# Transposes of the input powers later in TensorE's order, the state space's output products in halves of 64 rows, and a third bank for short products

## The chip, the cores and the metric

The kernel runs on one core of a Trainium2 chip. The metric is the device time of one execution in microseconds (us), the median of several. Engines are named as in the profile: PE is TensorE (PEld its weight loads), DVE is VectorE, ACT is ScalarE, POOL is GpSimd, SP is the engine that issues most DMAs.

## What is computed

A trunk of two layers on x of 512 tokens by 1024 channels. Each layer normalises its input, projects it, and runs three mixers side by side; their outputs are gated, merged and projected back. Cut to what matters here:

```python
for l in range(2):
    h = rmsnorm(x, norm_g[l])
    z = h @ w_in[l]                       # 1024 x 6656
    a_val, a_gate, b_val, b_gate, c_u, c_v, c_gate, gates = split(z)
    ya = s5_mixer(a_val, ...) * silu(a_gate)      # 32 groups x 64 complex states, scan over time
    yb = pool_mixer(b_val, ...) * silu(b_gate)    # means over trailing windows of 2, 4, 8, 16 tokens
    yc = sgu_mixer(c_u, c_v, ...) * silu(c_gate)  # 128 x 128 position mixing
    merged = sum(sigmoid(gates) * (ys @ w_branch[l]))
    x = x + merged @ w_out[l]
return rmsnorm(x, final_norm_g)
```

The kernel runs the scan of `s5_mixer` in blocks of 8 time steps. For that it needs, once for both layers, powers of the state matrix times the input gain (the "input powers", tile `ak`) and powers of a rotation (tables `tlo`, `thi`); then for each of four tiles of eight groups short products for the lags within a block (`psk`), the block states (`pse`) and the outputs (`psy`).

## The kernel before

Every large product is made in three passes of float32r: `hi*hi`, `lo*hi` and `hi*lo` (L104 to L106, helper `step`), so one block of 128 output channels over 1024 inputs is 24 matmuls of 128x512. The weights stream in as items: SP loads a raw tile `wr`, ACT rounds it to `wh` (L156), DVE subtracts to get `wl` (L157); each of the three has three buffers. An item whose PE work is done frees its `wh` and `wl` for the third item after it.

TensorE's order is the order in which the program is recorded. Beside the main stream run "sides": Python generators that record a few instructions, then yield a number of microseconds; `tick` (L132) resumes one when the recorder's own clock, which counts 0.64 for each step of three matmuls (`spend`), has passed that much. The side `s5_side` (L524) of layer 0 first copies tables (`stacked`), then makes the input powers: `input_powers` (L376) has six DVE operations into `ak` tiles (L384 to L387), four PE transposes into the bank `psa` (L390), an ACT copy (L392) and a DMA to HBM, `akd`; then come the rotations (L395), all on POOL, and then the four tiles. Where the side resumes, its PE instructions stand in TensorE's order, and TensorE works in order.

The orders of DVE, ACT, POOL and SP are not written by hand: a scheduler plays the recorded program through a timeline when the kernel is built and sets each engine's order by it, sides at a lower priority. Each engine then works in that order; an instruction that waits holds up all behind it on its engine.

Small tiles of up to 128x256 come from the pool `fs` of 8 buffers (L60, helper `small_spare`): the `ap` tiles of the powers of the state matrix, `ak`, the products `tb` of the rotations (L410), `bt`, the tables `tp`, `rt` and more. A request takes over the buffer of an earlier tile, and its first writer waits until that tile's last reader is done. So the order of the requests in the program decides who waits for whom. Short products share the PSUM pool `pa` (L65): `psb`, `psa`, `psk`, `psy`, `pss`, `psz`.

The main stream of layer 0 around the change is, in blocks of 24 matmuls: the four blocks of `a_val` (tile `u`), three blocks of the pooling branch on the unscaled input (called E1, E2, E3 below, operands `gh`, `gl`), its fourth block (P0, operands `hi`, `lo` of the scaled input `hf`, L670 to L673), four gate blocks G3, G2, G1, G0, each followed by a short product `psb` of three matmuls, then the merge: gate blocks O0, O1, then J0 (four steps on `hi`, `lo` of the pooling outputs `y`), O2, J1 and so on. POOL makes the pooled sums (`xq`, L744 to L748) from `xp` (L734), DVE turns them into `pt` (L751 to L753) and splits them (L434).

Of the kernel before, what the change touches and what calls it, by code (L numbers as in the profile page):

```python
# [13 lines left out]
PSUM = bass.MemoryType.PSUM  # L14

P = 128
# [4 lines left out]
NK = 64  # L21
# [4 lines left out]
GELU_A = 0.044715  # L26
GELU_B = 1.5957691216057308
SIDE = 1000
W_PREP = (75.0, 25.0)
W_OPS = 15.0  # L30
W_STATE = 5.0
W_OUT = 16.0
# [19 lines left out]
def hybrid_trunk(ctx: ExitStack, tc, xT, wi, wbr, wo, wglu, wmisc, pv, rows, gain, slam, sbc, sbt, cst, out):  # L52
    nc = tc.nc
    V, S, G, PE = nc.vector, nc.scalar, nc.gpsimd, nc.tensor
# [7 lines left out]
    bp = ctx.enter_context(tc.tile_pool(name="bp", bufs=1))  # L62
    kp = ctx.enter_context(tc.tile_pool(name="kp", bufs=24))
    pm = ctx.enter_context(tc.tile_pool(name="pm", bufs=4, space=PSUM))
    pa = ctx.enter_context(tc.tile_pool(name="pa", bufs=2, space=PSUM))  # L65
    pe = ctx.enter_context(tc.tile_pool(name="pe", bufs=1, space=PSUM))

    S.preload_act_table(AF.Sigmoid)
# [3 lines left out]
    def nm(s):  # L72
        count[0] += 1
        return f"{s}_{count[0]}"
# [4 lines left out]
    def spare(s="f", dt=F32, shape=(P, T)):  # L79
        return fp.tile(list(shape), dt, tag="f", name=nm(s))  # L80

    def small_spare(s="f", shape=(P, T // 2)):
        return fs.tile(list(shape), F32, tag="fs", name=nm(s))
# [4 lines left out]
    def aux(s="aux"):  # L88
        return pa.tile([P, T], F32, tag="aux", name=nm(s))
# [137 lines left out]
    def keep(s, shape):  # L227
        return cp.tile([P, *shape], F32, name=s)
# [84 lines left out]
    def k_unit(a, eng=V):  # L313
        ar, ai = a
        n = k32()
        eng.tensor_tensor(n, k_mul(ar, ar, eng), k_mul(ai, ai, eng), ALU.add)
        f = k32()
        eng.tensor_scalar(f, n, -0.5, 1.5, ALU.mult, ALU.add)
        return k_mul(ar, f, eng), k_mul(ai, f, eng)
# [46 lines left out]
    def stacked():  # L366
        for h in range(2):
            for r in range(2):
                a, b = slice(64 * r, 64 * r + 64), slice(64 * h, 64 * h + 64)
                for o, x, sign in ((war, apr, 1 - 2 * r), (wai, api, -1)):  # L370
                    S.activation(o[a].rearrange("p j (q h) -> p j h q", h=2)[:, :, h], x[b], AF.Copy, scale=float(sign))
                for o, x, sign in ((kar, kre, 1), (kai, kim, 2 * r - 1)):
                    S.activation(o[a].rearrange("p (q h) -> p h q", h=2)[:, h], x[b], AF.Copy, scale=float(sign))


    def input_powers():  # L376
        kr, ki = (bc(a, 1, NS) for a in (kre, kim))
        ar, ai = apr[:, 0:NS], api[:, 0:NS]
        v = lambda a: a.rearrange("p l s q -> p s l q")
        w = lambda a: a.rearrange("p s (l q) -> p s l q", l=DEPTH)  # L380
        ps = aux("psa")
        for r, (x, y, op) in enumerate(((ar, ai, ALU.subtract), (ai, ar, ALU.add))):
            p0, p1 = (small_spare("ak", (P, NS, W2)) for _ in range(2))
            V.tensor_tensor(p0, kr, x, ALU.mult)  # L384
            V.tensor_tensor(p1, ki, y, ALU.mult)
            ak = small_spare("ak", (P, DEPTH, NS, NQ))
            V.tensor_tensor(v(ak), w(p0), w(p1), op)  # L387
            for l in range(DEPTH):
                i = 2 * l + r
                PE.transpose(ps[:, i * P : (i + 1) * P], ak[:, l].rearrange("p s q -> p (s q)"), ident)  # L390
        t = spare("ak")
        S.activation(t, ps, AF.Copy)  # L392
        nc.sync.dma_start(akd.rearrange("l r p e -> p (l r) e"), t.rearrange("p (i e) -> p i e", i=4))

    def rotations(cn, sn):  # L395
        w = k_unit((cn, sn), G)
        for _ in range(3):
            w = k_unit(k_cmul(w, w, eng=G), G)
        for tab, n in ((tlo, 8), (thi, 8)):
            G.memset(tab[0][:, :, 0:1], 1.0)  # L400
            G.memset(tab[1][:, :, 0:1], 0.0)
            m = 1
            while m < n:
                wr = w[0].unsqueeze(2).to_broadcast([P, W2, m])
                wj = w[1].unsqueeze(2).to_broadcast([P, W2, m])
                tr, ti = tab[0][:, :, 0:m], tab[1][:, :, 0:m]
                ps = []
                for x, y in ((tr, wr), (ti, wj), (tr, wj), (ti, wr)):
                    o = small_spare("tb", (P, W2, m))
                    G.tensor_tensor(o, x, y, ALU.mult)  # L410
                    ps.append(o)
                G.tensor_tensor(tab[0][:, :, m : 2 * m], ps[0], ps[1], ALU.subtract)
                G.tensor_tensor(tab[1][:, :, m : 2 * m], ps[2], ps[3], ALU.add)
                w = k_unit(k_cmul(w, w, eng=G), G)
                m *= 2

    def bc(ap, axis, n):
        a = ap.unsqueeze(axis)
        shape = list(a.shape)
        shape[axis] = n  # L420
        return a.to_broadcast(shape)
# [15 lines left out]
    def flat(a):  # L437
        return a.rearrange("p q k -> p (q k)")
# [4 lines left out]
    tm = keep("tm", (8, P))  # L443
    hst = keep("hst", (8, NK))
# [79 lines left out]
    def s5_side(l, ud, st):  # L524
        uu = bp.tile([P, 4, 8, NK], F32, tag="ba", name=nm("uu"))
        for s in range(NS):
            r = 16 * (NS - 1 - s)
            src = ud.rearrange("n (g c) (s k) -> s c (n g) k", c=16, s=NS)[s]
            nc.sync.dma_start(uu[r : r + 16].rearrange("p n g k -> p (n g) k"), src)
        if l == 0:  # L530
            stacked()
            input_powers()
            yield 3
            rotations(*angle)
        ych = bp.tile([P, 4, T], F32, tag="bb", name=nm("ych"))
        st["ych"] = ych
        for t in range(4):
            w = s5_output(l, t)
            e = s5_input(l, t)
            tcs, tsn, rt = s5_tables(l, t)  # L540
            yield W_PREP[l] if t == 0 else W_OPS
            s5_lags(l, t, w)
            yield W_STATE
            ps = pe.tile([P, 2, 4, NK], F32, tag="pe", name=nm("pse"))
            for r in range(2):
                for i in range(4):
                    for h in range(2):
                        PE.matmul(ps[64 * h : 64 * h + 64, r, i], e[r][:, 2 * i + h], uu[:, t, 2 * i + h], start=True, stop=True)  # L548
            sr, si = flat(ps[:, 0]), flat(ps[:, 1])

            def mul(x, y, eng=V):
                o = small_spare("p5")
                eng.tensor_tensor(o, x, y, ALU.mult)  # L553
                return o

            a, b = mul(sr, tcs), mul(si, tsn)
            G.tensor_tensor(a, a, b, ALU.add)  # L557
            d, c = mul(si, tcs), mul(sr, tsn)
            V.tensor_tensor(d, d, c, ALU.subtract)
            gr, gi = small_spare("g5"), small_spare("g5")  # L560
            V.tensor_tensor_scan(gr, rt, a, 0.0, ALU.mult, ALU.add)
            V.tensor_tensor_scan(gi, rt, d, 0.0, ALU.mult, ALU.add)
            b, c = mul(gi, tsn, G), mul(gr, tsn, G)
            a, d = mul(gr, tcs), mul(gi, tcs)
            v3 = lambda z: z.rearrange("p (q k) -> p q k", q=4)[:, :, 0 : NK - 1]
            for r, (x, y, op) in enumerate(((a, b, ALU.subtract), (d, c, ALU.add))):
                for h in range(2):
                    o = hst[64 * r : 64 * r + 64].rearrange("p (q h) k -> p h q k", h=2)[:, h, :, 1:NK]
                    i = slice(64 * h, 64 * h + 64)
                    V.tensor_tensor(o, v3(x)[i], v3(y)[i], op)  # L570
            yield W_OUT
            py = aux("psy")
            for g in range(8):
                o = py[:, g * NK : (g + 1) * NK]
                PE.matmul(o, tm[:, g], uu[:, t, g], start=True, stop=False)  # L575
                PE.matmul(o, w[:, g, 16 : 16 + P], hst[:, g], start=False, stop=True)  # L576
            sq = spare("sq")
            S.activation(sq, py, AF.Square)
            V.tensor_scalar(sq, sq, GELU_A, 1.0, ALU.mult, ALU.add)
            V.tensor_tensor(sq, sq, py, ALU.mult)  # L580
            S.activation(sq, sq, AF.Sigmoid, scale=GELU_B)
            V.tensor_tensor(sq, py, sq, ALU.mult)
            yd = dp.tile([P, T], F32, tag="yd", name=nm("yd"))
            nc.sync.dma_start(yd, sq)
            for g in range(8):
                src = yd.rearrange("(s c) (g k) -> g c s k", c=16, g=8)[g]
                nc.sync.dma_start(ych[16 * g : 16 * g + 16, t].rearrange("p (s k) -> p s k", s=NS), src)
# [474 lines left out]
    with tc.high_priority(offset=-SIDE), tc.issue_after(norms[0].last[1]):  # L1062
        angle = discretise()
# [90 lines left out]
```

## Time and profile before

| | |
|---|---|
| median of 3 runs | 936.67 us (936.38 to 936.79) |
| the profiled execution | 937.1 us |
| its span in the profile | 935.3 us, so 1.8 us lie around it |
| PE busy | 890.3 us, 95% of the span |
| DVE, ACT, POOL busy | 579.1, 299.6, 227.9 us |
| granted TensorE clock, mean | 0.979 of full speed |

Of the page's 40 slices of 23.4 us PE is busy for 4 tenths in the second and third, for 6 tenths in the last and for 8 or more in all others. A busy PE is not PE at its peak: matmuls are pipelined, and their ends are modelled. So starts are compared below: two matmuls of 128x512 that follow each other start 0.227 us apart at full clock (0.43 us at half).

### The profile page before, as it was taken

To read this page: it belongs to the slowest core of one execution; us is meant where nothing else is said; L and a number is where in the kernel's file an instruction comes from. 1 tells how busy PE (TensorE), PEld (TensorE's weight loads), DVE (VectorE), ACT (ScalarE), POOL (GpSimd) and SP (SyncE) were. 2 spreads that over 40 slices of the span, in tenths; PEclk is the share of its full clock that TensorE was granted. 3 is DMA by queue.
4 is the path that set the end of the run, shared out by engine and by line. 5 is a ranking of instruction groups with operands and counts; after the bars stand their busy time and mean duration, and the time that the engine had idled before them with its cause. 6 is when DMAs were issued, how large, how long until landed. Compare 5 with 4: busy or idle time off the path is not lost.

```text
span 935.3 us, 11781 instructions
## 1 busy us (share of the span) xinstructions
PE 890.3 (95%) x4396; PEld 732.0 (78%) x4396; DVE 579.1 (62%) x934; ACT 299.6 (32%) x440; POOL 227.9 (24%) x353
## 2 busy tenths in 40 slices
PE   9449899999999999999999999999999999999996
PEld 5338688888888888888888788887888888888885
DVE  7875662787867776445547787566883435634632
ACT  5232322232222234333433333232322223433521
POOL 1068970213324340000230720201220111000020
PEclk9769899999999999999999999999999999999998
DMA  6823223453324444234225624354422332332402
GB/s 238 172 46 104 68 90 98 147 169 119 119 84 134 131 125 134 90 90 135 91 92 153 127 83 145 98 182 140 145 90 83 101 103 90 103 98 86 155 23 90
DMA packets 65704, 106.85 MB, mean 114 GB/s; under 512 B 30176, under 2 KB 32864, under 8 KB 65648
## 3 DMA queue, kind: packets, MB, share of 16 engines
q1 hardware_dynamic: 65008, 104.88, 37.6%
q0 software_dynamic: 352, 1.10, 0.4%
q8 instruction: 34, 0.56, 0.2%
q14 instruction: 22, 0.18, 0.1%
q10 hardware_dynamic: 288, 0.14, 0.1%
HBM read 99.01 MB, written 7.08 MB: 113 GB/s over the span
## 4 chain that ended last, share of the span: by engine, by line
PE 84%; DVE 8%; POOL 3%; DMA 2%; issue 2%; ACT 1%; SPq 0%; DVEq 0%; ACTq 0%
PE mm L104 23%; PE mm L105 23%; PE mm L106 23%; PE mm L1019 2%; PE mm L1020 2%; PE mm L1021 2%; PE mm L838 1%; PE mm L839 1%; PE mm L840 1%; PE psy L576 1%; PE psy L575 1%; POOL xq L744 1%; PE pse L548 1%; DVE wl L157 1%; PE mm L1015 1%
## 5 line engine op out<-in xcount | busy, mean ns | idle before, releaser
L104 PE MATMUL mm<-hi,wh 128*128 128x512 f32 x960 | 378.2, 394 | 1.0 <-ACT hi L672 1.0
L105 PE MATMUL mm<-lo,wh 128*128 128x512 f32 x960 | 374.8, 390 | 0.5 <-DVE lo L673 0.4
L106 PE MATMUL mm<-hi,wl 128*128 128x512 f32 x960 | 374.4, 390 | 0.1
L157 DVE TENSOR_TENSOR wl<-wr,wh 128x1024 fp32r<-128x1024 f32 (+1 forms) x174 | 200.4, 1152 | 155.7 <-ACT wh L156 155.3
L156 ACT ACTIVATE wh<-wr 128x1024 fp32r<-128x1024 f32 (+1 forms) x174 | 160.2, 921 | 416.7 <-PE mm L105 261.8
L104 PEld LDWEIGHTS mm<-hi,wh 128*128 128x128 f32 x960 | 180.8, 188 | 40.3 <-issue 1.9
L106 PEld LDWEIGHTS mm<-hi,wl 128*128 128x128 f32 x960 | 180.7, 188 | 38.5 <-DVE wl L157 0.5
L105 PEld LDWEIGHTS mm<-lo,wh 128*128 128x128 f32 x960 | 180.7, 188 | 38.3 <-DVE lo L673 0.8
L794 DVE TENSOR_TENSOR sg<-sg,mm 128x512 f32<-128x512 f32 x48 | 32.8, 684 | 44.4 <-PE mm L106 44.4
L796 POOL TENSOR_TENSOR sg<-sg,sg 128x512 f32<-128x512 f32 x16 | 25.2, 1577 | 101.7 <-DVE sg L794 101.7
L609 POOL TENSOR_TENSOR sq<-sq,sq 128x512 f32<-128x512 f32 x7 | 12.7, 1811 | 127.5 <-ACT sq L603 116.6
L104 PE MATMUL mm<-gh,wh 128*128 128x512 f32 x96 | 38.8, 405 | 0.1
L105 PE MATMUL mm<-gl,wh 128*128 128x512 f32 x96 | 38.1, 397 | 0.6 <-DVE gl L599 0.6
L106 PE MATMUL mm<-gh,wl 128*128 128x512 f32 x96 | 38.0, 396 | 0.4 <-DVE wl L162 0.4
L94 ACT ACTIVATE hi<-sg 128x512 fp32r<-128x512 f32 x32 | 20.2, 631 | 33.3 <-DVE sg L796 13.5
L557 POOL TENSOR_TENSOR p<-p,p 128x256 f32<-128x256 f32 x8 | 5.9, 739 | 91.2 <-DVE p L553 91.1
L785 ACT ACTIVATE sg<-mm 128x512 f32<-128x512 f32 x48 | 27.8, 579 | 0.0
L390 PE MATMUL psa<-cs,ak 128*128 128x128 f32 x4 | 1.3, 440 | 27.6 <-DVE ak L387 27.6
L95 DVE TENSOR_TENSOR lo<-sg,hi 128x512 fp32r<-128x512 f32 x32 | 22.0, 687 | 6.5 <-ACT hi L94 6.4
L838 PE MATMUL mm<-wh,hi 128*128 128x512 f32 x64 | 25.5, 398 | 0.2 <-DVE sg L794 0.2
L1019 PE MATMUL mm<-wh,hi 128*128 128x512 f32 x64 | 25.3, 396 | 0.0
L870 POOL TENSOR_TENSOR sg<-sg,z 128x512 f32<-128x512 f32 x8 | 14.6, 1820 | 44.1 <-DVE z L862 44.1
(207 smaller groups left out, 1064.9 us busy)
## 6 DMA issues: line engine op xcount, KB each, us to landing
wr<-in_wi SPq DMA_DIRECT2D x102, 512.0 KB, 3.2
wr<-in_wbr SPq DMA_DIRECT2D x48, 256.0 KB, 2.6
wr<-in_wo SPq DMA_DIRECT2D x16, 512.0 KB, 3.8
ai<-akd SPq DMA_DIRECT2D x16, 256.0 KB
bi<-in_sbt SPq DMA_DIRECT2D x16, 256.0 KB, 4.9
x<-in_xT SPq DMA_DIRECT2D x8, 256.0 KB, 5.2
ud<-u SPq DMA_DIRECT2D x8, 256.0 KB, 2.0
uu<-ud SPq DMA_DIRECT2D x16, 128.0 KB, 6.7
```

The costliest lines, as they stand in the source:

```text
L94: S.activation(hi, src, AF.Copy)
L95: V.tensor_tensor(lo, src, hi.bitcast(F32), ALU.subtract)
L104: PE.matmul(ps, whi[:, k], x[0], start=k == 0, stop=False)
L105: PE.matmul(ps, whi[:, k], x[1], start=False, stop=False)
L106: PE.matmul(ps, wlo[:, k], x[0], start=False, stop=k == n - 1)
L156: S.activation(hi, raw, AF.Copy)
L157: V.tensor_tensor(lo, raw, hi.bitcast(F32), ALU.subtract)
L785: S.activation(sg[m], ps, AF.Sigmoid)
L794: V.tensor_tensor(g, g, ps, ALU.mult)
L796: (V if last is not None else G).tensor_tensor(g, g, macc[m], ALU.add)
L838: PE.matmul(ps, th, w(wh), start=j == 0 and k == 0, stop=False)
L1019: PE.matmul(ps, th, w(wh), start=j == 0 and k == 0, stop=False)
```

## The change

Three edits, and the waits of the side's generator retuned with them.

1. In layer 0's side the rotations are recorded before the input powers, and the input powers only 32 of the recorder's microseconds later (`W_POWERS`); the wait before the first tile's lag products falls from 75 to 30.
2. The pool `pa` gets a third bank.
3. The output products `psy` are made in halves: instead of two products of 128 output rows for each of 8 groups, four of 64 rows. There are 8 such steps of 8 groups (four tiles, two layers).

```diff
--- before.py
+++ after.py
@@ -26,7 +26,8 @@
 GELU_A = 0.044715
 GELU_B = 1.5957691216057308
 SIDE = 1000
-W_PREP = (75.0, 25.0)
+W_POWERS = 32.0
+W_PREP = (30.0, 25.0)
 W_OPS = 15.0
 W_STATE = 5.0
 W_OUT = 16.0
@@ -62,7 +63,7 @@
     bp = ctx.enter_context(tc.tile_pool(name="bp", bufs=1))
     kp = ctx.enter_context(tc.tile_pool(name="kp", bufs=24))
     pm = ctx.enter_context(tc.tile_pool(name="pm", bufs=4, space=PSUM))
-    pa = ctx.enter_context(tc.tile_pool(name="pa", bufs=2, space=PSUM))
+    pa = ctx.enter_context(tc.tile_pool(name="pa", bufs=3, space=PSUM))
     pe = ctx.enter_context(tc.tile_pool(name="pe", bufs=1, space=PSUM))
 
     S.preload_act_table(AF.Sigmoid)
@@ -529,9 +530,10 @@
             nc.sync.dma_start(uu[r : r + 16].rearrange("p n g k -> p (n g) k"), src)
         if l == 0:
             stacked()
+            rotations(*angle)
+            yield W_POWERS
             input_powers()
             yield 3
-            rotations(*angle)
         ych = bp.tile([P, 4, T], F32, tag="bb", name=nm("ych"))
         st["ych"] = ych
         for t in range(4):
@@ -571,9 +573,12 @@
             yield W_OUT
             py = aux("psy")
             for g in range(8):
-                o = py[:, g * NK : (g + 1) * NK]
-                PE.matmul(o, tm[:, g], uu[:, t, g], start=True, stop=False)
-                PE.matmul(o, w[:, g, 16 : 16 + P], hst[:, g], start=False, stop=True)
+                for h in range(2):
+                    o = py[64 * h : 64 * h + 64, g * NK : (g + 1) * NK]
+                    PE.matmul(o, tm[:, g, 64 * h : 64 * h + 64], uu[:, t, g], start=True, stop=False)
+                for h in range(2):
+                    o = py[64 * h : 64 * h + 64, g * NK : (g + 1) * NK]
+                    PE.matmul(o, w[:, g, 16 + 64 * h : 80 + 64 * h], hst[:, g], start=False, stop=True)
             sq = spare("sq")
             S.activation(sq, py, AF.Square)
             V.tensor_scalar(sq, sq, GELU_A, 1.0, ALU.mult, ALU.add)
```

Lines of the changed kernel are up to five higher than those before (the transposes L390 are L391, the pooling L744 is L749).

**TensorE, from the end of layer 0's fourth `a_val` block (`mm_564`).** Before, the transposes stand right behind it, ahead of E1 (`mm_705`):

```order
L106 MATMUL mm_564<-gh_188,wl_465 128x512
L104 MATMUL mm_564<-gh_194,wh_464 128x512
L105 MATMUL mm_564<-gl_195,wh_464 128x512
L106 MATMUL mm_564<-gh_194,wl_465 128x512
L390 MATMUL psa_679<-cs,ak_684 128x128 x2
L390 MATMUL psa_679<-cs,ak_692 128x128 x2
L104 MATMUL mm_705<-gh_146,wh_520 128x512
L105 MATMUL mm_705<-gl_147,wh_520 128x512
L106 MATMUL mm_705<-gh_146,wl_521 128x512
```

With the change they stand behind G2 and its short product, ahead of G1 (`mm_1294`):

```order
L107 MATMUL mm_1230<-hi_639,wl_1138 128x512
L105 MATMUL psb_1258<-hi_1082,hi_1029 128x512
L106 MATMUL psb_1258<-lo_1083,hi_1029 128x512
L107 MATMUL psb_1258<-hi_1082,lo_1030 128x512
L391 MATMUL psa_1268<-cs,ak_1273 128x128 x2
L391 MATMUL psa_1268<-cs,ak_1281 128x128 x2
L105 MATMUL mm_1294<-hi_597,wh_1182 128x512
L106 MATMUL mm_1294<-lo_598,wh_1182 128x512
L107 MATMUL mm_1294<-hi_597,wl_1183 128x512
```

So 144 matmuls of 128x512 (E1 to E3, P0, G3, G2) and two short products moved ahead of the transposes. The first lag products moved from behind 468 large matmuls to behind 408.

**DVE, around the six operations that make `ak`** (the waits name the semaphore, by engine). Before, they follow the last steps of the discretisation:

```order
L363 TENSOR_TENSOR kim<-k_432,inv_417 128x32 [waits DVE_49]
L384 TENSOR_TENSOR ak_680<-kre,apr_107 128x256 [waits DVE_49]
L385 TENSOR_TENSOR ak_681<-kim,api_108 128x256 [waits DVE_49]
L387 TENSOR_TENSOR ak_684<-ak_680,ak_681 128x8x2x16 [waits DVE_49]
L384 TENSOR_TENSOR ak_688<-kre,api_108 128x256
L385 TENSOR_TENSOR ak_689<-kim,apr_107 128x256
L387 TENSOR_TENSOR ak_692<-ak_688,ak_689 128x8x2x16 [waits DVE_49]
L487 TENSOR_TENSOR w_363_1062<-war,sbc_1054 128x576 [waits DMAHW2_49,Activation_49]
L488 TENSOR_TENSOR m_364_1063<-wai,sbc_1054 128x576 [waits Activation_49]
```

With the change they follow the outputs of G3 and G2, and the first and the third of them wait for POOL:

```order
L654 TENSOR_TENSOR sg_1255<-sg_1255,mm_1230 128x512 [waits Activation_49]
L772 SCALAR_TENSOR_TENSOR y_1262<-psb_1258,pvt,sg_1255 128x512 [waits DVE_49,PE_49]
L96 TENSOR_TENSOR lo_1265<-y_1262,hi_1264 128x512 [waits Activation_49]
L385 TENSOR_TENSOR ak_1269<-kre,apr_107 128x256 [waits Pool_49]
L386 TENSOR_TENSOR ak_1270<-kim,api_108 128x256
L388 TENSOR_TENSOR ak_1273<-ak_1269,ak_1270 128x8x2x16 [waits DVE_49,Pool_49]
L385 TENSOR_TENSOR ak_1277<-kre,api_108 128x256
L386 TENSOR_TENSOR ak_1278<-kim,apr_107 128x256 [waits DVE_49]
L388 TENSOR_TENSOR ak_1281<-ak_1277,ak_1278 128x8x2x16 [waits DVE_49]
L478 TENSOR_TENSOR bt_1335<-sbc_1333,kar 128x128 [waits DMAHW1_49,PE_49]
L479 TENSOR_TENSOR bt_1336<-sbc_1333,kai 128x128 [waits Pool_49]
L488 TENSOR_TENSOR w_420_1341<-war,sbc_1333 128x576
```

Their buffers in `fs` are now taken over from the rotations' products `tb`: in the built program the first `ak` waits for L413 of POOL's second round on `thi` (tile 128x64), the third for L414 behind it, and the `bt` operation L479 for the third round (128x128). Before it was the other way round: `tb` waited for `ak`.

**POOL, at the start of the rotations** (the products L232 of `k` tiles, L233 with the change). Before, the rotations stand right behind the norm's `rs`, and the pooled sums `xq` stand among them:

```order
L412 TENSOR_TENSOR tlo_112<-tb_847,tb_849 128x32 [waits Pool_49]
L413 TENSOR_TENSOR tlo_113<-tb_851,tb_853 128x32 [waits Pool_49]
L309 TENSOR_TENSOR k_857<-k_859,k_861 128x32 [waits Pool_49]
L232 TENSOR_TENSOR k_864<-k_841,k_843 128x32
L232 TENSOR_TENSOR k_866<-k_843,k_841 128x32
L744 TENSOR_TENSOR xq_733<-xp_730 128x7x64 [waits DVE_49]
L745 TENSOR_TENSOR xq_733<-xp_730 128x64
L310 TENSOR_TENSOR k_858<-k_864,k_866 128x32 [waits Pool_49]
L232 TENSOR_TENSOR k_870<-k_857 128x32
L744 TENSOR_TENSOR xq_737<-xq_733 128x6x64 [waits Pool_49]
```

With the change all pooled sums of layer 0 stand first, then four memsets of tiles of layer 1, and then the rotations:

```order
L749 TENSOR_TENSOR xq_1169<-xp_1166 128x7x64 [waits Activation_49,Pool_49]
L750 TENSOR_TENSOR xq_1169<-xp_1166 128x64 [waits Pool_49]
L736 MEMSET xp_4685 128x8 [waits DVE_49]
L746 MEMSET xq_4688 128x8
L746 MEMSET xq_4692 128x8 [waits DVE_49,Pool_49]
L736 MEMSET xp_4747 128x8
L233 TENSOR_TENSOR k_680<-k_370 128x32
L233 TENSOR_TENSOR k_682<-k_362 128x32
L317 TENSOR_TENSOR k_679<-k_680,k_682 128x32 [waits Pool_49]
```

The third of those memsets waits until DVE has done L758 (before L753) on the last of the four `pt`. The rotations stand behind it.

## Rows read from the trace of the kernel before

**Rows 1.** The page: span, and a group of part 5 (xcount | busy us, mean ns).

```profile
span 935.3 us, 11781 instructions
...
L157 DVE TENSOR_TENSOR wl<-wr,wh 128x1024 fp32r<-128x1024 f32 (+1 forms) x174 | 200.4, 1152 | 155.7 <-ACT wh L156 155.3
```

**Rows 2.** Waits of PE: engine line waited for: us in total, times, longest us.

```profile
PE psa L390 <- DVE ak L387: 27.6, 2, 27.1
PE psb L104 <- DVE y L767: 4.1, 1, 4.1
```

**Rows 3.** Timeline of PE, 32 to 127 us: start us, us, engine line op xcount [idle before].

```profile
32.42 0.39 PE L106 MATMUL mm<-gh,wl 128*128 128x512 f32 x1
59.90 0.66 PE L390 MATMUL psa<-cs,ak 128*128 128x128 f32 x2 [27.09 <-DVE ak L387]
...
61.39 0.78 PE L104 MATMUL mm<-gh,wh 128*128 128x512 f32 x1
...
67.91 0.39 PE L104 MATMUL mm<-gh,wh 128*128 128x512 f32 x1
...
126.77 0.50 PE L105 MATMUL mm<-lo,wh 128*128 128x512 f32 x1
```

**Rows 4.** Timeline of DVE, 33 to 61 us.

```profile
33.20 0.74 DVE L670 SCALAR_TENSOR_TENSOR hf<-x,pvt,rstd 128x512 f32<-128x512 f32 x1
...
50.32 0.68 DVE L673 TENSOR_TENSOR lo<-hf,hi 128x512 fp32r<-128x512 f32 x1
...
55.77 0.18 DVE L232 TENSOR_TENSOR k<-api,lam 128x32 f32<-128x32 f32 x1
...
58.50 0.41 DVE L384 TENSOR_TENSOR ak<-kre,apr 128x256 f32<-128x256 f32 x1
...
60.57 0.43 DVE L387 TENSOR_TENSOR ak<-ak,ak 128x256 f32<-128x256 f32 x1
```

**Rows 5.** Timeline of DVE, 74 to 86 us.

```profile
76.44 1.58 DVE L157 TENSOR_TENSOR wl<-wr,wh 128x1024 fp32r<-128x1024 f32 x1
...
83.37 1.01 DVE L752 TENSOR_TENSOR xq<-xq,cs 128x16 f32<-128x16 f32 x1
...
85.39 1.09 DVE L434 TENSOR_TENSOR lo<-pt,hi 128x512 fp32r<-128x512 f32 x1 [0.76 <-ACT hi L433]
```

**Rows 6.** Timeline of POOL, 53 to 117 us.

```profile
53.27 0.50 POOL L232 TENSOR_TENSOR k<-k 128x32 f32<-128x32 f32 x2 [24.76 <-DVE k L232]
...
68.60 0.27 POOL L410 TENSOR_TENSOR tb<-tlo,k 128x32 f32<-128x32 f32 x1
...
112.42 0.25 POOL L309 TENSOR_TENSOR k<-k,k 128x32 f32<-128x32 f32 x1
...
113.38 0.44 POOL L232 TENSOR_TENSOR k<-k 128x32 f32<-128x32 f32 x2
...
114.96 0.31 POOL L410 TENSOR_TENSOR tb<-thi,k 128x64 f32<-128x64 f32 x1
...
116.43 0.32 POOL L412 TENSOR_TENSOR thi<-tb,tb 128x64 f32<-128x64 f32 x1
```

**Rows 7.** Timeline of PE around the first `pse` and `psy` steps.

```profile
162.65 0.39 PE L106 MATMUL mm<-hi,wl 128*128 128x512 f32 x1
162.97 0.69 PE L548 MATMUL pse<-uu,e 128*64 128x64 f32 x16
...
164.05 0.50 PE L104 MATMUL mm<-hi,wh 128*128 128x512 f32 x1
164.39 0.39 PE L105 MATMUL mm<-lo,wh 128*128 128x512 f32 x1
...
183.00 0.39 PE L106 MATMUL mm<-hi,wl 128*128 128x512 f32 x1
183.23 0.33 PE L575 MATMUL psy<-uu,tm 128*128 128x64 f32 x2
...
187.03 0.40 PE L839 MATMUL mm<-wl,hi 128*128 128x512 f32 x1
```

## The prediction

> **What bounds the kernel now.** I read the page first, then the waits of PE, then the timelines of PE, DVE and POOL where PE stands. The span is 935.3 us [rows 1], the profiled execution 937.1; the sum below is made against the latter, and the median of the runs lies 0.4 lower. PE is the bound: its waits after the start are two that matter, 27.6 us before the transposes `psa` and 4.1 us before one short product `psb` [rows 2]. In its timeline the reader sees the last matmul of the `a_val` blocks start at 32.42, nothing until the transposes at 59.90, and then 24 matmuls that take 6.52 us (61.39 to 67.91) where 24 at 0.227 take 5.45 [rows 3]: the clock is at its lower level at first, which costs 1.1 us. The other end of this wait is DVE's: from 33.20 it splits the scaled input (last `lo` at 50.32) and beside it computes the powers of the state matrix, and makes `ak` from 58.50 to 61.0 [rows 4]. E1 to E3 need none of this, yet stand behind the transposes. So the first edit takes away a wait that is plainly there. What it costs is the question, since the six `ak` operations get new neighbours.
>
> **When `ak` comes now.** Until L758 on the last `pt`, DVE has its old work and 25 operations that stood behind `ak` before. The old work, from 33.20 to the product L232 of `api` and `lam` that is done at 55.95 [rows 4], is 22.75 us. Moved ahead of that are 6 `wl` (1.15 us in the mean [rows 1], up to 1.58 [rows 5]), 3 `xp`, 4 `pt`, 3 `lo` and the `lo` of `wq` (each a pass over 128x512 like the `lo` of 0.68 [rows 4]; the pooled `lo` up to 1.09 [rows 5]), 4 corrections of 16 columns (0.2 like other small operations [rows 4], up to 1.01 beside POOL [rows 5]) and 4 small `pt` (0.2). All low that is 6.9 + 11 x 0.68 + 8 x 0.2 = 16.0; all high 9.5 + 8 x 0.68 + 3 x 1.09 + 4.0 + 0.8 = 23.0. POOL works on `xq` for about half of that time, and most of these operations keep their duration then, so I take 18. DVE also waits 0.5 for E1, whose result is there at 38.3 (32.65 + 5.45 + 0.2) when DVE would take it at 37.9 by its old pace. That gives 55.95 + 18 + 0.5 = 74.5 (72.5 to 79.5).
>
> Only then POOL's held memset is free, and the rotations begin at 74.7, where before they began at 53.27 [rows 6]. The first `ak` waits for their second round on `thi`. Where DVE leaves POOL alone, normalising a rotation takes 1.58 (113.38 to 114.96) and squaring and normalising 3.05 (112.42 to 114.96, and half a microsecond for the first pair, which stands beside other work there); the round of 64 columns takes 1.8 to its L412 (114.96 to 116.75) [rows 6], 4.6 in all. By these, and 0.3 less and 0.7 more for 32 and 128 columns, the way to the release is 1.58 + 3 x 3.05 for the start, then 4.3 + 4.6 + 5.3 for `tlo`, 4.3 and 1.8 for `thi`: 31.0 us. In the trace of before the start alone, 10.7 by this, took 15.3 (53.27 to 68.60 [rows 6]), beside a DVE that worked nearly all the time: 1.43 times as long, and 44.3 for the whole if that held throughout. It should not hold: with the change DVE has only some 12 us of work left before it stands at `ak` itself, and then nothing disturbs POOL. I add 2.2 for those 12 us and take 33.2, nearest to the undisturbed rows. The release comes at 107.9, and the six `ak`, 2.5 us as now (58.50 to 61.0 [rows 4]), are done at 110.4.
>
> **What PE makes of it.** E1 to E3 run from 32.65 at full pace, P0 waits for the last `lo` (some 6 us later than now, at about 57), G3 and G2 follow, and PE stands before the transposes at about 70: a wait of 40 us for 31.7 before. From the end of `ak`: 0.4 to the first matmul and 6.5 for G1 (as E1 behind the same transposes, 61.0 to 61.39 to 67.91 [rows 3]), 0.7 for its `psb`, 5.45 for G0, 0.7, and 10.9 for O0 and O1: 24.65 us, so J0 starts at 135.0. Before, it started at 126.5 (its second matmul waits until 126.77 [rows 3]). From there PE has work without a gap in both kernels, so the first edit costs **8.5 us**. I cost what lies behind `ak` on DVE at nothing: the lag tables, the first input tiles through HBM and the outputs of G1 and G0 must be ready for J0, and by the same durations they are some 2 us early in those 24.65; three more would show as a wait of 1. The third bank costs nothing and removes the wait of 4.1, which is for a bank that `y` still held; that is in the two start times already. The shorter `W_PREP` brings the lag products 60 matmuls nearer; they come 16 us after J0, behind tables that are finished by then.
>
> **The output products.** A `psy` step now is 32 passes (8 of the rows of 2, for each operand) and takes 3.58: from 183.00 to 187.03, less two matmuls of 0.227 [rows 7]. A `pse` step has passes of the new shape, 64 columns by 64, the halves in turn: 32 of them from 162.97 to 164.05, 1.08, and 1.29 with the gaps on both sides (162.65 to 164.39, less two matmuls) [rows 7]. The new `psy` has 64: 1.29 + 1.08 = 2.37. Eight steps gain 8 x 1.21 = **9.7 us**, all on PE's path. Ends: no gain at all if a half pass costs half of the present 0.11, and at best 18.3 if a step fell to `pse`'s 1.29; `pse` is the same shape and order, so I take its pace.
>
> The sum is 8.5 - 9.7 = -1.2 us: 935.9 for the profiled execution, 935.5 as a median.
>
> **The rivals.**
> *The halves overlap less over a long step* (slower). A step of 64 passes is twice as long as any run of such passes in this trace, and what stands queued at its start may hide the loads of 32 but not of 64. If loads set the pace, two halves cost what one whole does, 0.11 a pair, and `psy` stays at 3.5: the gain is nil, and 8.5 us remain: 945.2. It decides at a pace of 0.054 a pass; `pse` at 0.034 speaks against it, its shortness leaves it open. The Trainium skill, "TensorE: Matmul & The Clock Gate", section "LDWEIGHTS (loading the stationary operand)", says that a load takes its number of columns divided by 1.2 in nanoseconds; an estimate by that page is 64 loads of 53 ns, 3.4 us a step, so nearly this case. By that rule, `pse` would take 1.7 where the trace has 1.08 [rows 7], so the loads of the two halves overlap at least there.
> *POOL stays as slow as before* (slower). At 1.43 times its undisturbed pace throughout the rotations take 44.3, `ak` is done at 121.5, J0 starts 19.6 late, and the sum is +9.9: 946.6. For it: POOL was slow wherever it ran beside DVE [rows 6]; against it: DVE stands still from about 86.
> *The transposes do not wait for POOL* (much faster). If the buffers came free earlier, DVE would go on at about 86, `ak` would be done at 88.5 and J0 start 13.4 early: -23 with the halves, 913.6. Against it stand the waits in the built order; POOL would have to do 31 us of work in 12.
>
> **How the numbers follow.** The forecast has a chance of 0.62, the halves without gain 0.15, the slow POOL 0.13, no wait for POOL 0.05; 0.05 is left for what I don't see. The forecast's own range comes from the start of the rotations (72.5 to 79.5), their pace (31 upwards) and a step of `psy` between 2.2 and 2.8: 930.5 to 941. To hold 8 in 10 the range goes up into the two slower rivals: 930.5 to 945.5. A difference of 0.2%, 1.9 us, is about what a measurement of this kernel can tell from none. The forecast lies within it, near its lower side: of its 0.62, I put 0.26 to faster, 0.22 to no change and 0.14 to slower. The slower rivals add 0.22 to slower and 0.06 to the others, the fast one and half of the rest go to faster. That is 0.36 faster, 0.28 no change, 0.36 slower.
>
> **What would show it.** PE's waits have one long one, about 40 us, before the transposes, by DVE's `ak`; DVE's first `ak` stands some 20 us waiting for POOL's L413; POOL begins the rotations at about 75 and runs faster from 86 on; J0's first matmul is near 135; the wait of 4.1 before `psb` is gone; a `psy` step takes about 2.4. The prediction is wrong if `ak` is done before 100 or after 118, or if a `psy` step is near 3.5.

## The result and the profile after

The changed kernel takes 941.46 us as the median of 4 runs (941.37 to 944.0), the kernel before beside it 936.54 (936.38 to 936.79). The ratio is 1.0059 with a 95% interval of 1.0041 to 1.0076: slower by 4.9 us, where 1.2 us less were forecast. The profiled execution took 941.43 us, its span is 939.6, which is 4.3 more than before [rows 1]. Lines of the page, with the slices of PE and of its granted clock:

```profile
span 939.6 us, 12276 instructions
...
PE 882.9 (94%) x4652; PEld 719.5 (77%) x4652; DVE 578.1 (62%) x934; ACT 299.9 (32%) x440; POOL 216.0 (23%) x353
...
PE   9981199999999999999999999999999999999996
...
PEclk9986599999999999999999999999999999999998
```

In the row of PE the gap is now in one piece, slices 4 and 5, and the clock row shows 6 and 5 tenths of full speed granted there. PE is busy for 882.9 us, 7.4 less than before. The waits of PE (engine line waited for: us in total, times, longest):

```profile
PE psa L391 <- DVE ak L388: 38.8, 2, 38.2
PE mm L105 <- ACT hi L677: 2.8, 4, 1.0
PE mm L106 <- DVE lo L678: 1.4, 3, 0.8
PE mm L107 <- DVE wl L158: 1.3, 1, 1.3
PE mm L843 <- DVE sg L799: 1.2, 1, 1.2
```

Against [rows 2] the wait of 4.1 before `psb` is gone, and that before `psa` has grown from 27.6 to 38.8. DVE's timeline says what `ak` waited for:

```profile
88.12 0.80 DVE L96 TENSOR_TENSOR lo<-y,hi 128x512 fp32r<-128x512 f32 x1 [0.69 <-ACT hi L95]
110.96 0.53 DVE L385 TENSOR_TENSOR ak<-kre,apr 128x256 f32<-128x256 f32 x1 [22.03 <-POOL thi L413]
...
113.28 0.43 DVE L388 TENSOR_TENSOR ak<-ak,ak 128x256 f32<-128x256 f32 x1
...
117.01 0.53 DVE L479 TENSOR_TENSOR bt<-sbc,kai 128x128 f32<-128x128 f32 x1 [3.05 <-POOL thi L413]
```

DVE is done with all else at 88.9, and then stands 22 us before the first `ak`, for POOL's `thi`. Where before `ak` was done at 61.0 [rows 4], it is now at 113.71. The same stretch of POOL:

```profile
72.96 0.11 POOL L746 MEMSET xq<- 128x8 f32 x1
77.72 0.11 POOL L746 MEMSET xq<- 128x8 f32 x1 [4.64 <-DVE pt L758]
...
77.81 0.93 POOL L233 TENSOR_TENSOR k<-k 128x32 f32<-128x32 f32 x2
...
110.60 0.32 POOL L413 TENSOR_TENSOR thi<-tb,tb 128x64 f32<-128x64 f32 x1
```

A memset waits at 77.72 for the last `pt` of DVE, the rotations begin behind it at 77.81 (53.27 before [rows 6]), and the round that releases `ak` ends at 110.92, 33.1 us later. On PE this gives:

```profile
73.93 0.39 PE L107 MATMUL psb<-hi,lo 128*128 128x512 f32 x1
112.53 0.69 PE L391 MATMUL psa<-cs,ak 128*128 128x128 f32 x2 [38.22 <-DVE ak L388]
...
114.10 0.78 PE L105 MATMUL mm<-hi,wh 128*128 128x512 f32 x1
...
118.51 0.63 PE L106 MATMUL mm<-lo,wh 128*128 128x512 f32 x1
118.94 0.44 PE L107 MATMUL mm<-hi,wl 128*128 128x512 f32 x1
...
121.99 0.39 PE L105 MATMUL psb<-hi,hi 128*128 128x512 f32 x1
...
128.11 0.39 PE L105 MATMUL psb<-hi,hi 128*128 128x512 f32 x1
...
139.67 0.39 PE L105 MATMUL mm<-hi,wh 128*128 128x512 f32 x1
```

PE has run E1 to E3, P0, G3 and G2 by 74.3. The row at 112.53 is the transposes, 114.10 the first matmul of G1, 118.51 and 118.94 the last two that start at the half-clock spacing of 0.43; 121.99 and 128.11 are the `psb` of G1 and G0, 139.67 is J0. Before, J0's first matmul stood at 126.31 and its second waited until 126.77 [rows 3]; I count its start as 126.5, one matmul ahead of the second. So everything up to J0 costs 13.2 us.

The output products, to be held against [rows 7]:

```profile
182.39 0.39 PE L107 MATMUL mm<-hi,wl 128*128 128x512 f32 x1
182.70 0.34 PE L578 MATMUL psy<-uu,tm 128*64 128x64 f32 x4
182.87 0.29 PE L581 MATMUL psy<-hst,w 128*64 128x64 f32 x4
...
184.50 0.29 PE L581 MATMUL psy<-hst,w 128*64 128x64 f32 x4
184.72 0.50 PE L105 MATMUL mm<-hi,wh 128*128 128x512 f32 x1
185.05 0.39 PE L106 MATMUL mm<-lo,wh 128*128 128x512 f32 x1
```

The 64 passes stand in groups of four, 0.117 apart, so 0.029 a pass; all eight steps show the same. From 182.39 to 185.05, less two matmuls of 0.227, a step takes 2.21 where it took 3.58: 1.37 less, eight times 11.0. After J0 the waits of PE come to 4.9 us (1.3 + 1.2 + 1.0 + 0.9 + 0.5), before to 2.4. So the difference adds up: 13.2 - 11.0 + 2.5 = 4.7, where the spans differ by 4.3.

### The profile page after: what moved, and what is told of

The parts are those of the page before. It is cut to its first block, busy times and chain, and to the rows that moved or that the text cites. A ratio compares the mean times of both kernels' runs of the same rounds, so it can differ in the third digit from the quotient of the medians.

```text
span 939.6 us, 12276 instructions
## 1 busy us (share of the span) xinstructions
PE 882.9 (94%) x4652; PEld 719.5 (77%) x4652; DVE 578.1 (62%) x934; ACT 299.9 (32%) x440; POOL 216.0 (23%) x353
## 4 chain that ended last, share of the span: by engine, by line
PE 86%; DVE 6%; POOL 3%; DMA 2%; issue 2%; ACT 1%; SPq 0%; DVEq 0%; ACTq 0%
PE mm L105 24%; PE mm L106 24%; PE mm L107 24%; PE mm L1024 2%; PE mm L1025 2%; PE mm L1026 2%; PE mm L843 1%; PE mm L844 1%; PE mm L845 1%; DVE wl L158 1%; POOL k L233 1%; PE pse L550 1%; DVE hf L675 1%; PE psy L578 1%; PE psz L865 1%
## 5 line engine op out<-in xcount | busy, mean ns | idle before, releaser
L158 DVE TENSOR_TENSOR wl<-wr,wh 128x1024 fp32r<-128x1024 f32 (+1 forms) x174 | 198.4, 1141 | 159.8 <-ACT wh L157 159.2
L391 PE MATMUL psa<-cs,ak 128*128 128x128 f32 x4 | 1.4, 447 | 38.8 <-DVE ak L388 38.8
L391 PEld LDWEIGHTS psa<-cs,ak 128*128 128x128 f32 x4 | 0.6, 202 | 39.6 <-DVE ak L388 39.6
L843 PE MATMUL mm<-wh,hi 128*128 128x512 f32 x64 | 25.4, 397 | 1.2 <-DVE sg L799 1.2
L844 PE MATMUL mm<-wl,hi 128*128 128x512 f32 x64 | 25.1, 392 | 0.9 <-DVE wl L158 0.9
```

Of the source, the lines that this page charges most:

```text
L158: V.tensor_tensor(lo, raw, hi.bitcast(F32), ALU.subtract)
L843: PE.matmul(ps, th, w(wh), start=j == 0 and k == 0, stop=False)
L844: PE.matmul(ps, th, w(wl), start=False, stop=False)
```

## Experiments

Ratios are to the kernel before, run beside it on the same chip (its medians there were 936.0 to 936.6).

**The three edits one by one.** First the halves alone:

```diff
+                for h in range(2):
+                    o = py[64 * h : 64 * h + 64, g * NK : (g + 1) * NK]
+                    PE.matmul(o, tm[:, g, 64 * h : 64 * h + 64], uu[:, t, g], start=True, stop=False)
...
```

> The kernel before with nothing changed but the psy step in halves of 64 rows. By the traces of before and of the change a psy step with its gaps went from 3.58 to 2.21 us, 1.37 less, and there are eight: theory one (the halves are a pure gain on TensorE's path, and the late waits of the changed kernel come from its new order) gives 936.5 - 11.0 = 925.5. Rival (the halves bring the 2.5 us of late waits of the changed kernel with them, because the products that follow come sooner): 928. Rival (a step that is faster only in the changed kernel's places, nil here): 936.5.

928.24 us, ratio 0.992 (0.9897 to 0.9944). The runs lie between 926.7 and 931.7, so the interval is wide; the profiled one has a span of 924.9, 10.4 below before, and its waits of PE are those of before but for some 0.5 us. A step takes 2.21 here too. So the halves are worth 11.0 us of TensorE's path, and the time keeps most of it. A product of the second layer (L841, on DVE's `sg`, at 628.7) waits 1.2 us, where before the longest such wait was 0.2; so one of the late waits comes with the halves, as the first rival has it. Its reason is another one, though: in this trace DVE first stands 6.6 us for an input tile from HBM (`ai`, at 621.39) and does the last operation on it (L466) just ahead of that `sg`, where before it ended 8.4 us ahead of it.

Then the new order with the third bank, and `psy` whole (the third edit undone):

> The changed kernel with its psy step whole again: new order and third bank alone. Theory one (J0 starts 13.2 us later because ak waits for POOL's rotations, and the order brings 2.5 us of late waits): 936.5 + 13.2 + 2.5 = 952, with J0's first matmul near 139.7. If the late waits belong to the halves: 949.7. If the order itself costs nothing and the halves are what is slow: 937 or less.

948.12 us, ratio 1.0119 (1.0104 to 1.0135): 11.5 us slower. The wait before `psa` is 39.5, and J0 starts near 138.5 (the second `psb` behind the transposes is at 126.95, and 0.68 and 48 matmuls of 0.227 lie between). So the order is what costs: 12.0 us at J0, 10.7 in the span (946.0 against 935.3). It brings no more late waits by itself (2.1 us after J0, 2.4 before), so 949.7 was the nearest of the three. In the spans the order and the halves alone come to 10.7 - 10.4 = 0.3 us, together they cost 4.3. Of the 4.0 between, 1.2 is the later J0 (the lower clock, see below), 1.5 are longer waits for `wl` after it; the rest wasn't followed.

Then the third bank alone on the kernel before:

```diff
-    pa = ctx.enter_context(tc.tile_pool(name="pa", bufs=2, space=PSUM))
+    pa = ctx.enter_context(tc.tile_pool(name="pa", bufs=3, space=PSUM))
```

> The kernel before with a third bank for short products and nothing else. If the wait of 4.1 us before psb at 102 to 106 is a wait for a bank that y holds, it goes, and with it some 1 us of lower clock behind it: J0 near 121.5 and 931.5. Rival (the bank is held by a chain that the next product meets as well, so the wait moves by one place): 936.5, with a wait of 3 to 5 us before the following psb or J0.

936.85 us, ratio 1.0005 (0.9996 to 1.0015): nothing. The rival is right, and the trace shows the new place. The waits of PE, then DVE's timeline, then three rows of DVE in the kernel before:

```profile
PE psa L390 <- DVE ak L387: 27.5, 2, 27.0
PE mm L104 <- ACT hi L94: 5.2, 1, 5.2
```

```profile
112.71 0.75 DVE L767 SCALAR_TENSOR_TENSOR y<-psb,pvt,sg 128x512 f32<-128x512 f32 x1
116.66 0.39 DVE L477 TENSOR_TENSOR bt<-sbc,kar 128x128 f32<-128x128 f32 x1 [3.21 <-POOL thi L412]
...
122.09 0.74 DVE L767 SCALAR_TENSOR_TENSOR y<-psb,pvt,sg 128x512 f32<-128x512 f32 x1
125.38 1.17 DVE L95 TENSOR_TENSOR lo<-y,hi 128x512 fp32r<-128x512 f32 x1 [2.54 <-ACT hi L94]
```

```profile
105.26 0.75 DVE L767 SCALAR_TENSOR_TENSOR y<-psb,pvt,sg 128x512 f32<-128x512 f32 x1
...
116.79 0.40 DVE L477 TENSOR_TENSOR bt<-sbc,kar 128x128 f32<-128x128 f32 x1 [3.20 <-POOL thi L412]
...
122.23 0.74 DVE L767 SCALAR_TENSOR_TENSOR y<-psb,pvt,sg 128x512 f32<-128x512 f32 x1
```

No `psb` waits any more, but J0 waits 5.2 us for the `hi` of the last `y`. On DVE a `bt` stands 3.2 us for POOL's `thi`, and the `y` that J0 needs comes behind it, at 122.09. In the kernel before, the same `bt` stands as long and the same `y` comes at 122.23; J0 lost only 0.2 to it there, as the wait for the bank, which a `y` at 105.26 ended, had already held TensorE up. So there are two waits one behind the other, the second for POOL's rotations, and the third bank takes away the first alone.

**Taking away the wait for POOL.** In the changed kernel, the six tiles of `ak` come from the pool of full-size tiles, so their buffers are not those of the rotations' products:

```diff
-            p0, p1 = (small_spare("ak", (P, NS, W2)) for _ in range(2))
+            p0, p1 = (spare("ak")[:, 0:256].rearrange("p (s w) -> p s w", s=NS) for _ in range(2))
...
-            ak = small_spare("ak", (P, DEPTH, NS, NQ))
+            ak = spare("ak")[:, 0:256].rearrange("p (l s q) -> p l s q", l=DEPTH, s=NS)
```

> The changed kernel, but the six tiles of ak come from the pool of full-size spare tiles, so that DVE no longer waits for POOL's products of the rotations. Theory one (this wait is what makes the order costly): ak is done near 84 where it was done at 113.7, TensorE's long wait falls from 38.2 to about 10 us, J0 starts near 111 and, if the lag products find their tables in time, the time is 941.5 - 28 = 913; POOL's tables may come late then, for up to 7 us: 913 to 920. Rival (POOL's rotations are the true end of this stage, and the wait only moves on to the lag and state products): 935 to 941.

917.23 us, ratio 0.9791 (0.9776 to 0.9805): 24 us faster than the changed kernel, 19 faster than before. Its waits:

```profile
PE psa L391 <- DVE ak L388: 9.9, 2, 9.4
PE mm L105 <- ACT wh L157: 3.1, 1, 3.1
PE mm L107 <- DVE wl L158: 2.5, 2, 2.1
```

The wait before `psa` has fallen from 38.2 to 9.4. From the first lag products to the first state products TensorE now takes 11.8 us (126.21 to 137.99) where it took 6.3 (156.08 to 162.36): 3.6 of the 5.5 are waits for `wh` and `wl`, the rest is lower clock behind them; the other 2.1 for a `wl` come at 325.0. This run settles the main question: the order was costly because of the shared buffers, and the end of POOL's rotations was no bound of its own.

The rest of that wait goes when `bt` and `rt` come from the same pool. First on the kernel before with its third bank:

```diff
-        p0, p1 = (small_spare("bt", (P, 4, 2, 16)) for _ in range(2))
+        p0, p1 = (spare("bt")[:, 0:128].rearrange("p (i h c) -> p i h c", i=4, h=2) for _ in range(2))
...
-        rt = small_spare("rt", (P, 4, NK))
+        rt = spare("rt")[:, 0 : 4 * NK].rearrange("p (q k) -> p q k", q=4)
```

> The kernel before with the third bank, and with the tiles bt and rt taken from the pool of full-size spare tiles. With the third bank alone the wait of 4.1 us before psb went and one of 5.2 before J0 came, for the last y, which stands on DVE behind a bt that waits for POOL's rotations. If that is what held y in both kernels: J0 starts some 5.6 us of waits and 1 us of lower clock earlier, 930 us. Rival (y is late by DVE's own work): 935 to 937.

929.61 us, ratio 0.9926 (0.9911 to 0.994). J0 no longer waits for `hi`; the only wait left there is 1.1 us for a `lo`. So bank and tiles together are worth 6.5 us, where the bank alone was worth nothing; the tiles alone weren't run.

The same two tiles on the kernel of `ak` from spare tiles:

> The kernel of ak from full-size spare tiles (917.2 us), with bt and rt from there as well, so that neither DVE nor ACT waits for the rotations before the tables of the scan. In its trace TensorE still lost 5.6 us between the first lag products and the first state products, by weights and state inputs that were late. If they were late by bt's wait for POOL: 911 to 913. Rival (spare tiles are too few now, and what is gained is lost to waits for those): 916 to 920.

911.8 us, ratio 0.9737 (0.9722 to 0.9751), as the first theory has it: from the first lag products to the first state products TensorE takes 6.3 us again.

Then the transposes further back:

```diff
-W_POWERS = 32.0
+W_POWERS = 42.0
```

> The same, with the transposes 10 us further back in TensorE's order (10 more of its budget, so behind G1 as well), where ak is already done when TensorE comes to them. The wait of 9.4 us before them should go, with some 1.5 us of lower clock behind it: 900 to 903 if nothing else is late. Rival (the wait turns up again at the next product that DVE feeds, psb of G1 or G0, since y stands behind the same work of DVE): 908 to 913.

910.67 us, ratio 0.9728 (0.9712 to 0.9745), not clearly different from the last. The rival is right. The waits of PE:

```profile
PE psa L391 <- DVE y L772: 3.4, 1, 3.4
PE mm L106 <- DVE lo L96: 3.3, 1, 3.3
...
PE mm L105 <- ACT hi L95: 1.4, 1, 1.4
```

The 9.2 before `psa` are 3.4 now, but J0 waits 3.3 and another matmul 1.4 for the halves of `y`: DVE is behind in this stretch, whichever of its products TensorE asks for first.

**The start of the rotations.** In the changed kernel, the memsets of the second layer's pooling tiles, behind which the rotations stand, go to DVE:

```diff
-                G.memset(xp[:, :, 0:PAD], 0.0)
+                (V if l else G).memset(xp[:, :, 0:PAD], 0.0)
...
-                        G.memset(nx[:, :, 0:PAD], 0.0)
+                        (V if l else G).memset(nx[:, :, 0:PAD], 0.0)
```

> The changed kernel with the memsets of the pooling tiles' pads of the second layer on DVE, so that POOL's rotations no longer stand behind memsets that wait for the last pt of the first layer. The rotations should begin near 72 where they began at 77.8. Theory one (ak, and so J0, follows the rotations one for one): 941.5 - 5.5 = 936, if DVE slows the first rounds by no more than it did; 938 if it takes half of that back. Rival (ak is held by DVE's own work): 941.

937.81 us, ratio 1.002 (1.0006 to 1.0034), 3.7 below the changed kernel. POOL's timeline:

```profile
72.44 0.57 POOL L233 TENSOR_TENSOR k<-k 128x32 f32<-128x32 f32 x2 [0.73 <-DVE k L233]
...
107.96 0.33 POOL L413 TENSOR_TENSOR thi<-tb,tb 128x64 f32<-128x64 f32 x1
```

The rotations begin 5.4 us earlier, and the release comes at 108.29, only 2.6 earlier: they take 35.9 us instead of 33.1, beside a DVE that still works at first. J0 gains a little more than the release: the `psb` of G0 starts at 124.19, 3.9 earlier, as the way from the transposes to the `psb` of G1 takes 8.2 us (109.89 to 118.06) where it took 9.5; the full clock is granted again 3.8 us after the first transpose, not 6.5. So `ak` and J0 do follow the rotations, and half of the head start is lost on the way.

**Why the halves are fast.** On the kernel before, the same 64 passes, but first all of the lower rows, then all of the upper:

```diff
-            for g in range(8):
-                o = py[:, g * NK : (g + 1) * NK]
-                PE.matmul(o, tm[:, g], uu[:, t, g], start=True, stop=False)
-                PE.matmul(o, w[:, g, 16 : 16 + P], hst[:, g], start=False, stop=True)
+            for h in range(2):
+                for g in range(8):
+                    o = py[64 * h : 64 * h + 64, g * NK : (g + 1) * NK]
...
```

> The kernel before with psy in halves, but first all 32 passes of the lower 64 rows and then all 32 of the upper, so that the halves never take turns. In the kernel with halves in turn a step took 64 passes at 0.029 us each. If this pace comes from the two halves of the array being loaded and run side by side, a step goes back to 3.4 to 3.7 us and the time to 936 to 938. If a pass of 64 columns simply costs about half of one of 128, the step stays near 2.2 and the time at 926 to 929.

940.02 us, ratio 1.0042 (1.0027 to 1.0056): slower than whole products.

```profile
182.74 0.39 PE L106 MATMUL mm<-hi,wl 128*128 128x512 f32 x1
183.06 0.33 PE L576 MATMUL psy<-uu,tm 128*64 128x64 f32 x2
183.22 0.28 PE L577 MATMUL psy<-hst,w 128*64 128x64 f32 x2
183.34 0.28 PE L576 MATMUL psy<-uu,tm 128*64 128x64 f32 x2
...
184.74 0.33 PE L576 MATMUL psy<-uu,tm 128*64 128x64 f32 x4
...
187.09 0.39 PE L840 MATMUL mm<-wl,hi 128*128 128x512 f32 x1
```

Now two passes take 0.117, 0.058 each, but for the four at 184.74 where the halves change over, and a step takes 3.90 (182.74 to 187.09, less 0.45). So the gain is not in the smaller pass: it is there only where two passes that follow each other make different halves of the output rows. The single starts in the traces rule out two other causes: that a pass adds onto the result of the one ahead of it, and that two passes in a row read the same input. In this run each pass starts 0.058 behind the last, adding or not, and only 0.006 behind where the half changes, at 184.74. And `pse`, whose two halves read different inputs, starts them 0.006 and 0.052 apart in turn, much as the `psy` of the changed kernel does (0.007 and 0.051). A step is dearer here than I expected (3.4 to 3.7), by 8 x 0.32 = 2.6 us over whole products; the time is 4.0 over, and the wait of 1.2 for `sg`, behind 6.8 us of DVE for `ai`, stands in this trace too, so it doesn't come from products that follow sooner.

**The rest.** Old order, third bank, `bt` and `rt` from spare tiles, and the halves:

> The kernel before with its old order, the third bank, bt and rt from full-size spare tiles, and psy in halves. The third bank with those tiles gave 929.6, and eight steps at 1.37 less are 11.0, of which the kernel with halves alone kept 8.4 by its time and 10.4 by its profile: 919 to 921. If this is at or below 911 the new place of the transposes is worth nothing; if it is near 920, the place is worth some 9 us once nothing waits for POOL.

921.79 us, ratio 0.9844 (0.9827 to 0.986). Beside 910.67 for the new place of the transposes, with the same other parts and `ak` apart, the place is worth 11 us. And two banks instead of three, in the changed kernel and in the fastest:

> The changed kernel with two banks for short products. If the third bank is covered by the 38 us that TensorE stands before the transposes (two psb are made before it, two behind): 941 to 943, no change. If a psb behind the transposes waits for y, as in the kernel before: 944 to 946.

945.24 us, ratio 1.0085 (1.0059 to 1.0111), against 1.0059 (1.0041 to 1.0076) with three: the intervals overlap. No `psb` waits, and the second one behind the transposes starts at 128.36 (128.11 with three). The first expectation holds up to J0; what lies above 943 in three of its four runs is by its trace 1.7 us more of waits for `wl` and some 1.6 of lower clock behind one of them (349.8 to 354.9); what makes `wl` late stays open.

> The fastest kernel so far (910.7 us) with two banks for short products. There four psb stand at a distance of 6 us and DVE makes y late, so the bank should count here: a wait of 3 to 6 us before the third or fourth psb, 914 to 917. If y frees the banks in time: 911.

909.03 us, ratio 0.9711 (0.9694 to 0.9729): no difference from three banks that can be shown. One `psb` does wait for `y`, 3.4 us, but DVE's `y` is what TensorE would wait for at J0 otherwise. So the third bank counts in neither, and the version to keep is this one or that with three: 25 to 27 us, 2.7 to 2.9%, faster than the kernel before.

## Why the prediction was wrong

**What stands behind `ak` was right.** The prediction said that the transposes would wait for `ak`, this for POOL's L413, some 20 us (22.0), and PE some 40 (38.2); that the rotations would need 33.2 us from start to release (33.1), and that the wait before `psb` would go. The wait for POOL is shown by the run that takes it away. The rivals fell: POOL kept its pace, the halves overlap over a long step, and the transposes did wait. (PE was there at 74.3 and not at 70; the wait covers that.) So 941.5 lies in the stated range of 930.5 to 945.5 without either of the two rivals for which its upper part was there; it is above the forecast's own 930.5 to 941. The sum failed in its terms:

**The start of the rotations was 3.1 us off.** The step that failed is DVE's old work, taken over at 22.75 us as if it kept its duration, in the estimate of 74.7 for POOL's held memset. From 33.0 to the last `pt` at 77.5 DVE works or waits for 44.5 us: 1.0 of that is idle, 7.2 are six more `wl`, 7.5 the operations on `xp`, `pt` and `wq`. So the new work is 14.7 us, less than the 18 that I allowed for it; but the rest, the old work, is 28.8, and was 21.8 (22.75 less 1.0 idle), as POOL now works beside it where it was idle until 53.27 [rows 6]. Thirteen operations in this stretch take 0.2 to 0.95 us longer than the same kind took before beside an idle POOL, and POOL works for 0.93 or more of each; twelve others beside POOL keep their time. Rows of DVE, then of POOL, in the changed kernel:

```profile
39.40 1.65 DVE L675 SCALAR_TENSOR_TENSOR hf<-x,pvt,rstd 128x512 f32<-128x512 f32 x1
...
48.24 1.64 DVE L675 SCALAR_TENSOR_TENSOR hf<-x,pvt,rstd 128x512 f32<-128x512 f32 x1
...
51.84 0.74 DVE L675 SCALAR_TENSOR_TENSOR hf<-x,pvt,rstd 128x512 f32<-128x512 f32 x1
```

```profile
38.86 1.64 POOL L749 TENSOR_TENSOR xq<-xp 128x448 f32<-128x448 f32 x1 [10.54 <-DVE xp L739]
...
47.69 1.63 POOL L749 TENSOR_TENSOR xq<-xp 128x448 f32<-128x448 f32 x1 [0.56 <-DVE xp L739]
```

The same `hf` of 128x512 takes 0.74 when POOL is idle (51.84), as all eight did before, and 1.65 and 1.64 beside POOL's sums, in which it ends only after POOL's first long operation has (40.50 and 49.32). The Trainium skill, "SBUF — State Buffer", section "Who interferes with whom", says that a DVE instruction with two SBUF inputs contends with a GpSimd instruction that reads SBUF, and that the one that comes second is blocked until the first is done. By these rows the trace agrees so far: `hf` ends 0.55 and 0.56 us behind POOL's operation, a little less than the 0.74 it takes alone; no run here varied it alone. I had charged POOL with DVE's presence (its rotations slower by 2.2 us) and not DVE's old work with POOL's, though the rows for it were at hand: 1.58 for a `wl` and 1.01 for a small `xq` beside POOL [rows 5].

**The way from `ak` to J0 was 1.3 us off.** I took 6.5 us for G1, as E1 had behind the same transposes [rows 3]; it took 7.9 (114.10 to 121.99). In its timeline matmuls follow each other at 0.43, the spacing of the 1.2 GHz level, up to 118.94 (114.67 is the first), where 24 matmuls lost 1.1 before and 2.4 now. The stand ahead of it was 38 us and not 27, but the longer stand is not the reason. With the order alone TensorE stood 39.5 us, full clock was granted again 3.7 us after the first transpose, and G1 took 6.6; in the run of earlier rotations it was 36.4, 3.8 and 6.6. Here the full clock came after 6.5 us, in the kernel before after 3.6, and with the third bank alone, behind a stand of 27.0, after 5.4. So the 6.5 held in some runs and not in others, and what decides it stays open.

**The output products gained 11.0 instead of 9.7**, since a step fell to 2.21 and not 2.37. The pace of `pse` (0.034) was the right neighbour, and a long run is a little faster (0.029). The Trainium skill's page on loads that the prediction weighed ("TensorE: Matmul & The Clock Gate", section "LDWEIGHTS (loading the stationary operand)") gives an estimate of 53 ns for each pass of 64 columns; the run whose halves don't take turns shows 58, so that rule comes near for one half at a time and fails for two in turn. The Trainium skill, "TensorEngine Tiling (Array Packing)", section "Key Properties", says that tiles of the array load and multiply in parallel; the two paces here, 0.029 in turn and 0.058 not, agree.

**The late waits after J0 were not in the sum.** I wrote that from there PE has work without a gap in both kernels. They grew from 2.4 to 4.9 us: 2.2 more for `wl`, whose lateness wasn't followed, and 1.0 more for the `sg` that comes with the halves, while 0.8 fell away. In all, against the forecast of -1.2: +3.1 for the start, +0.2 for `ak`, +1.3 for the clock, -1.3 for the halves, +2.5 for the late waits, 4.6 in place of the 4.3 measured in the span. The start is the largest term; three of one sign made a small gain a small loss.

**The third bank** was costed at nothing, with the wait of 4.1 counted in J0's start. No run shows it worth anything in this kernel; alone it only lets TensorE come to the next wait.

## What to carry to other kernels

When a program records one engine's work before another's and both take buffers from one small pool, ask for each first writer which engine must still read the buffer: here POOL's 33 us came to stand before six operations of DVE through nothing but the order of the requests, and another pool for six small tiles was worth 24 us. A wait for a bank can hide a later one: the third bank alone was worth nothing, as the next wait, for POOL, ended at about the same time, and 6.5 us once that was taken away too. Look for what the engine meets next before paying for buffers. Before moving work of one engine beside another's, price the slowing in both directions, from rows where the two already run side by side.

## What the runs showed of the hardware

Products of 64 rows in two halves that take turns run at 0.029 us a pass, and at 0.058 when one half follows itself: the order of recording alone was worth 12 us here (928.2 against 940.0). Two of DVE's operations on 128x512 took 2.2 times as long beside POOL's sums (1.65 and 1.64 against 0.74). And TensorE's clock, at 0.5 behind a stand, came back 3.6 to 6.5 us after work began again, and not in the order of the stands: 3.7 behind 39.5 us, 6.5 behind 38.2, 3.8 behind 36.4, 5.4 behind 27.0 and 3.6 behind 27.1. Where TensorE is the bound, as here, that is up to 1.3 us between runs of the same order.
